# The first modulation of a two-block transformer found by four column tiles on TensorE, and GpSimd left out of the first four column blocks

## The chip, the cores and the metric

The kernel runs on one core of a Trainium2 chip. The metric is device time in microseconds of one execution. The profile is one execution, taken by the hardware profiler; its times count from the first instruction.

## The reference

Two transformer blocks work on x, [256 tokens, 1024 features], in float32. What matters here is the start of the first layer:

```python
mod = jax.nn.silu(c) @ ada_w + ada_b                 # [6144], from c [1024]
sh_m, sc_m, gt_m, sh_f, sc_f, gt_f = split(mod, 6)   # 1024 each
h = rms_norm(x, norm_mix) * (1 + sc_m) + sh_m        # rms_norm: x / sqrt(mean(x*x) + eps) * gain
proj = h @ w_in                                      # then attention, a gated delta net, ...
```

So before the first product `h @ w_in` can be finished, 2048 of the 6144 columns of `silu(c) @ ada_w` are needed (shift `sh_m`, scale `sc_m`): 8 MB of weights for one token's vector.

## The kernel before

x lies on chip by features: eight tiles X[k] of [128 features, 256 tokens]. Each float32 product is made of three float32r passes: a weight `w` is split into `wh` (rounded, by ScalarE, L193) and `wl` (the remainder, L194, by VectorE or GpSimd), and h likewise into `hh` and `hl`; L209, L210 and L211 are the three matmuls `wh hh`, `wh hl`, `wl hh`.

`begin0` starts the first layer. `Turn` squares X[k] on ScalarE (L65), adds the squares up on GpSimd (L67), and sums them over the features on TensorE (L81, tile `nps`); `rstd` (L290, L293) and `spread` (L271, L272) make 1 / rms, which ScalarE copies to `rb` (L465). Then four rounds j = 0..3 follow. Each round loads two units of ada_w (`mod_unit`, 1 MB each): VectorE multiplies [128 columns, 1024] by silu(c), which was spread over all partitions (`sc`, L458 and L459), and adds along the row (L346), twice a unit; L349 adds the bias, L352 makes the gain. The round also loads a weight block (0.5 MB) and cuts it, for j < 3 with the remainder on GpSimd; `norm` makes two blocks of h: the product with `rb` on GpSimd (L303), gain and shift on ScalarE (L305), `hh` on ScalarE (L308), `hl` on GpSimd (L309). Then TensorE multiplies what is there: in round j, weight blocks 0..j-1 with the two new blocks of h, and weight block j with all blocks of h so far.

Behind the four rounds `mixer1` goes on with token-major products (`pm`, L234 to L236), more column blocks (`pf`), convolutions (`gdn_conv`) and the gates' columns (`gps`, L658). A framework places the tiles and orders each engine's instructions ahead of time; on the chip each engine runs its own list strictly in that order, and waits where an operand isn't there. SyncE (SP) issues the loads in order too; a load waits until its buffer is free (five buffers for units of ada_w, three for weight blocks).

Of the kernel before, what the change touches and what calls it, by code (L numbers as in the profile page):

```python
# [17 lines left out]
P = 128          # partitions  # L18
S = 256          # tokens
SE = S + 2       # tokens and, beside them, columns for the shift  # L20
KT = 8           # feature blocks of the model width
NF = 22          # feature blocks of a feed-forward width
# [3 lines left out]
SENT = -3.4e38   # marks the scores that the top-64 search has taken  # L26

# columns of the packed constants
# [13 lines left out]
# columns of the packed norm gains: eight per norm  # L42
# [3 lines left out]
class Turn:  # L46
    """From one phase to the next.  step(k) follows the last update of x's feature block k and adds its squares;
    then(ms) follows the last of them, with the sums of each token, [128 tokens, 2]."""
# [48 lines left out]
class Start(Turn):  # L97
    """The next phase's h is x * gain, without the 1 / rms that all of x decides: that factor (net.rb along the free
    axis, net.rcol per partition) comes on the products, the first two of which run while it is found.  A shift rides
    along as columns beside the tokens: W' shift stands beside each product."""  # L100
# [42 lines left out]
class Net:  # L143
    """x lives on chip as eight [128 features, 256 tokens] tiles.  A float32 product is done as three
    float32r passes: both operands are split exactly into a rounded part and its remainder."""
# [29 lines left out]
    def parts(self, pool, name, n):  # L175
        """Two lists of a tile per feature block: the rounded parts and the remainders."""
        return [[pool.tile([P, n], F32R, name=f"{name}{i}{k}") for k in range(KT)] for i in "hl"]

# [18 lines left out]
    def split(self, src, hi, lo, scale=None):  # L197
        """hi + lo = src (times a column), both float32r."""
# [14 lines left out]
    def proj_fm(self, w, pool=None, tag="pj", n=S, between=None, h=None, bufs=2):  # L213
        """PSUM [128 columns, n] = W' h, for a [128, 8, 128] block of W."""
# [8 lines left out]
    def proj_tm(self, outs, src, n, pre=None):  # L223
        """outs[tb] [128 tokens, n] = h' W, for W as [2, 128, 4, n]."""
# [16 lines left out]
    def blocks(self, src, i0, n=2, pool=(), ws=None):  # L241
        """PSUM [128 columns, 256 tokens] of n blocks of columns."""
# [10 lines left out]
    def first(self, src, eng=None):  # L253
        """The first two blocks of a phase, loaded and split ahead."""
        ws = self.load(src, (P, 2, KT, P))
        return [self.cut(ws[:, j], eng=eng) for j in range(2)]

# [1 line left out]
    def warm(self, func, after):  # L259
        """Has the activation table of func loaded once the column `after` is there."""  # L260
# [3 lines left out]
    def spread(self, r, psum):  # L264
        """PSUM [128, 256]: r [128 tokens, 2] along the free axis, on every partition."""
# [9 lines left out]
    def rsqrt(self, y, x, t):  # L275
        """y = 1 / sqrt(x), by Newton's steps from the halved exponent, to float32's rounding."""
# [8 lines left out]
    def rstd(self, ms, eps=None, then=None):  # L285
        """1 / sqrt(ms / 1024 + eps); ms: [128 tokens, 2]."""
# [9 lines left out]
    def norm(self, ks, gain, shift, pool, act, rest):  # L296
        """h = x * rstd * gain + shift, split into hh + hl; gain and shift: [128, 8] columns.  The blocks whose product
        GpSimd does, whose gain and shift ScalarE, and whose remainder GpSimd: the others go to VectorE."""
# [12 lines left out]
    def final(self, ms, psum, gain, dst=None):  # L311
        """x = x * rstd * gain, kept or written out."""
# [13 lines left out]
    def two_norms(self):  # L326
        """The second block's first norm straight from the first block's x: with y = x g1 / sqrt(a + eps),
        a = mean(x^2), the norm of y is x g1 g2 / sqrt(mean(x^2 (g1^2 + eps)) + eps^2)."""
# [116 lines left out]
    def begin0(self, w_fm, pp):  # L445
        """The first layer's h by feature blocks, as their modulation comes in, and beside it four blocks of columns."""
        nc, tc, io = self.nc, self.tc, self.io
        with tc.tile_pool(name="st", bufs=1) as sp:
# [12 lines left out]
            for k in range(KT):  # L461
                t.step(k)
# [1071 lines left out]
```

## Time and profile before

| | |
|---|---|
| three timed runs | 1507.74, 1509.89, 1514.95 us |
| median | 1509.89 us |
| profiled execution, first to last instruction (its span) | 1508.1 us |
| TensorE matmuls busy in the span | 1429.1 us (95%) |
| VectorE, ScalarE, GpSimd busy | 1163.1, 841.9, 183.1 us |
| GpSimd busy from 18 to 46 us | 27.7 us of 28 |
| TensorE busy from 18 to 46 us | 9.7 us of 28 |

The profile gives the profiled execution no time of its own beside this span. Over the whole span TensorE is nearly always busy; the first 55 us are the exception, and the change lies there.

### The profile page before, as it was taken

How to read it: one execution, taken by the hardware profiler on the slowest of the kernel's cores; microseconds unless marked ns; L12 is line 12 of the kernel's file. 1: busy time of each engine (PE TensorE's matmuls, PEld its weight loads, DVE VectorE, ACT ScalarE, POOL GpSimd, SP SyncE). 2: the span in 40 equal slices, each digit the busy share in tenths (PEclk: the TensorE clock that was granted, in tenths of full speed). 3: DMA queues.
4: the chain of work that ended last, by engine and by line, in shares of the span. 5: the costliest groups of instructions: out<-in, count | busy, mean ns of one | idle time of the engine just before them, and what ended most of it. 6: DMA issues, size and time to landing. Idle time of an engine off the chain costs nothing.

```text
span 1508.1 us, 27966 instructions
## 1 busy us (share of the span) xinstructions
PE 1429.1 (95%) x11162; PEld 1350.4 (90%) x11162; DVE 1163.1 (77%) x2319; ACT 841.9 (56%) x1604; POOL 183.1 (12%) x164
## 2 busy tenths in 40 slices
PE   3888899999998899999999999999999999999998
PEld 2877789999997788999999988989999888899997
DVE  6879879999968565986567796698788665897875
ACT  3735775544465667654446555475555654765554
POOL 7434101000042410100001000110000100100000
PEclk9999999999999999999999999999999999999999
DMA  8567447898823522688844434179673332565520
GB/s 325 194 228 240 155 159 278 341 324 328 317 105 105 182 90 71 223 304 154 287 175 138 168 130 151 56 278 217 236 259 130 122 130 85 224 223 193 199 85 29
DMA packets 52500, 287.96 MB, mean 191 GB/s; under 512 B 6061, under 2 KB 11953, under 8 KB 24466
## 3 DMA queue, kind: packets, MB, share of 16 engines
q1 hardware_dynamic: 50962, 279.89, 50.8%
q0 software_dynamic: 1408, 6.29, 3.5%
q8 instruction: 87, 1.43, 0.4%
q14 instruction: 43, 0.35, 0.1%
HBM read 278.23 MB, written 7.34 MB: 189 GB/s over the span
## 4 chain that ended last, share of the span: by engine, by line
PE 76%; DVE 14%; POOL 4%; ACT 3%; issue 3%; DMA 1%; POOLq 0%; DVEq 0%; ACTq 0%
PE pf L209 14%; PE pf L210 14%; PE pf L211 14%; PE acc L209 5%; PE acc L211 5%; PE acc L210 5%; DVE wl L194 2%; DVE ws L346 2%; PE ot L415 2%; PE sc L377 2%; DVE hl L205 1%; POOL sq L67 1%; PE tp L408 1%; POOL h L303 1%; PE sc L376 1%
## 5 line engine op out<-in xcount | busy, mean ns | idle before, releaser
L210 PE MATMUL pf<-hl,wh 128*128 128x256 f32 (+1 forms) x2008 | 571.8, 285 | 12.3 <-DVE hl L205 7.3
L209 PE MATMUL pf<-hh,wh 128*128 128x256 f32 (+1 forms) x2008 | 576.8, 288 | 5.8 <-ACT hh L308 4.6
L211 PE MATMUL pf<-hh,wl 128*128 128x256 f32 (+1 forms) x2008 | 570.3, 285 | 10.9 <-POOL wl L194 9.2
L193 ACT CAST wh<-ws 128x1024 fp32r<-128x1024 f32 (+1 forms) x303 | 311.5, 1036 | 184.1 <-PE pf L210 133.8
L194 DVE TENSOR_TENSOR wl<-ws,wh 128x1024 fp32r<-128x1024 f32 (+1 forms) x290 | 356.1, 1231 | 70.5 <-ACT wh L193 69.2
L210 PEld LDWEIGHTS pf<-hl,wh 128*128 128x128 f32 x2008 | 382.9, 191 | 18.5 <-DVE hl L205 10.6
L211 PEld LDWEIGHTS pf<-hh,wl 128*128 128x128 f32 x2008 | 382.4, 191 | 12.4 <-POOL wl L194 9.8
L209 PEld LDWEIGHTS pf<-hh,wh 128*128 128x128 f32 x2008 | 382.4, 191 | 10.2 <-ACT hh L308 4.9
L211 PE MATMUL acc<-ah,dl 128*128 128x256 f32 x704 | 198.2, 282 | 0.0
L210 PE MATMUL acc<-al,dh 128*128 128x256 f32 x704 | 198.0, 282 | 0.0
L209 PE MATMUL acc<-ah,dh 128*128 128x256 f32 x704 | 197.7, 283 | 0.2
L67 POOL TENSOR_TENSOR sq<-sq 128x256 f32<-128x256 f32 x59 | 50.7, 859 | 786.4 <-ACT sq L65 780.3
L194 DVE TENSOR_TENSOR dl<-wd,dh 128x1024 fp32r<-128x1024 f32 x88 | 107.6, 1223 | 48.4 <-ACT dh L193 48.2
L193 ACT CAST dh<-wd 128x1024 fp32r<-128x1024 f32 x88 | 91.9, 1048 | 90.9 <-PE acc L210 87.5
L210 PEld LDWEIGHTS acc<-al,dh 128*128 128x128 f32 x704 | 133.7, 190 | 0.2
L211 PEld LDWEIGHTS acc<-ah,dl 128*128 128x128 f32 x704 | 133.6, 190 | 0.0
L209 PEld LDWEIGHTS acc<-ah,dh 128*128 128x128 f32 x704 | 132.9, 190 | 0.7 <-ACT ah L201 0.6
L346 DVE SCALAR_TENSOR_TENSOR ws<-ws,sc 128x1024 f32<-128x1024 f32 x96 | 121.4, 1278 | 4.7 <-DMA ws<-in_ada_w 4.7
L1069 DVE SCALAR_TENSOR_TENSOR fy<-fu,cw,fy 128x255 f32<-128x255 f32 (+1 forms) x176 | 84.1, 481 | 5.7 <-ACT fy L1067 3.0
L388 ACT ACTIVATE lg<-lg,st 128x128 f32<-128x128 f32 x112 | 49.8, 447 | 23.0 <-DVE st L383 15.4
L194 POOL TENSOR_TENSOR wl<-ws,wh 128x1024 fp32r<-128x1024 f32 x13 | 34.9, 2688 | 224.3 <-ACT wh L193 224.3
L1050 DVE TENSOR_TENSOR a<-pf,rb 128x258 f32<-128x258 f32 x88 | 37.1, 424 | 31.5 <-PE pf L211 29.3
(368 smaller groups left out, 2286.4 us busy)
## 6 DMA issues: line engine op xcount, KB each, us to landing
ws<-in_ada_w SPq DMA_DIRECT2D x48, 1024.0 KB, 6.4
ws<-in_w_gu SPq DMA_DIRECT2D x44, 1024.0 KB, 6.0
wd<-in_w_dn SPq DMA_DIRECT2D x44, 1024.0 KB, 6.7
ws<-in_w_up SPq DMA_DIRECT2D x44, 1024.0 KB, 4.8
ws<-in_w_fm SPq DMA_DIRECT2D x16, 1024.0 KB, 5.1
ws<-in_w_even SPq DMA_DIRECT2D x12, 1024.0 KB, 4.8
w<-in_cmp_w SPq DMA_DIRECT2D x8, 1024.0 KB, 4.8
ws<-in_w_out SPq DMA_DIRECT2D x8, 1024.0 KB, 4.8
```

The costliest lines, as they stand in the source:

```text
L67: (nc.vector if i else nc.gpsimd).tensor_tensor(sq, sq, last, op=ALU.add)
L193: nc.scalar.copy(wh, ws)
L194: (eng or nc.vector).tensor_tensor(wl, ws, wh.bitcast(F32), op=ALU.subtract)
L209: mm(out, lhsT=lh, rhs=rh, start=start, stop=False, **kw)
L210: mm(out, lhsT=lh, rhs=rl, start=False, stop=False, **kw)
L211: mm(out, lhsT=ll, rhs=rh, start=False, stop=stop, **kw)
L346: nc.vector.scalar_tensor_tensor(a, a, 1.0, self.sc, op0=ALU.mult, op1=ALU.mult, accum_out=acc)
L377: nc.tensor.matmul(sc[:, 128:384], lhsT=q[:, 128:256], rhs=kz, start=True, stop=True)
L388: nc.scalar.activation(lg[:, rng[i]], lg[:, rng[i]], AF.Exp, bias=nm[:, i:i + 1], scale=-1.0, accum_out=den[:, i:i + 1])
L415: mm(out, lhsT=v0, rhs=pt[:, 0:256], start=start, stop=False, skip_group_check=True)
L1050: nc.vector.tensor_tensor(t[j], ps[j], self.rb, op=ALU.mult)
L1069: nc.vector.scalar_tensor_tensor(y[:, d:S], u[:, 0:S - d], w[:, 2 - d:3 - d], y[:, d:S], op0=ALU.mult, op1=ALU.add)
```

## The change

Comments are left out. `io["ada_q"]` holds the first 2048 columns of ada_w of layer 0 again, in eight pieces of 1 MB with the 1024 inputs on partitions, so that they can be the moving operand of a matmul; a column of silu(c), padded to 32 columns with zeros (`cz`), is the stationary one. Each of the eight matmuls of a round takes one piece of 128 inputs and the same 512 columns (256 of the shift, 256 of the scale); the four of one load write to partitions 0, 32, 64 and 96 of one tile (`mrow`), the four of the second load add to them. A copy to SBUF and four matmuls with a column of ones (`mcol`) sum the four partial rows and turn them into columns.

```diff
+    def mod_rows(self, sp, pp, j, cz):
+        nc = self.nc
+        ps = pp.tile([P, 512], F32, tag="g", name="mrow", bufs=3)
+        for i in range(2):
+            aw = self.load(self.io["ada_q"][j, i], (P, 4, 512), sp, tag="aq", bufs=5)
+            for k in range(4):
+                q = slice(32 * k, 32 * k + 32)
+                nc.tensor.matmul(ps[q, :], lhsT=cz[:, 4 * i + k, :], rhs=aw[:, k, :], start=i == 0, stop=i == 1,
+                                 skip_group_check=True)
+        row = sp.tile([P, 512], F32, tag="mrow", name="mrow", bufs=2)
+        nc.scalar.copy(row, ps)
+        mp = pp.tile([P, 2, 2], F32, tag="s", name="mcol")
+        for i in range(4):
+            nc.tensor.matmul(mp[:, i // 2, i % 2:i % 2 + 1], lhsT=row[:, i * P:i * P + P], rhs=self.one, start=True,
+                             stop=True)
+        b = slice(2 * j, 2 * j + 2)
+        two = lambda t: t[:, 0, 0:16].rearrange("p (a b) -> p a b", a=2)[:, :, b]
+        nc.vector.tensor_tensor(two(self.mod), mp, two(self.adab), op=ALU.add)
+        nc.vector.scalar_tensor_tensor(self.gmod[:, 0, 0, b], self.mod[:, 0, 8 + 2 * j:10 + 2 * j], 1.0,
+                                       self.nrm[:, N_MIX + 2 * j:N_MIX + 2 * j + 2], op0=ALU.add, op1=ALU.mult)
...
     def begin0(self, w_fm, pp):
...
+            ct = sp.tile([P, KT], F32, name="ct")
+            nc.sync.dma_start(ct, io["c_cols"])
+            nc.sync.dma_start(self.x, io["x"])
             row = sp.tile([1, 1024], F32, name="row")
             nc.sync.dma_start(row, io["c"])
-            nc.sync.dma_start(self.x, io["x"])
             nc.sync.dma_start(self.adab, io["ada_b"])
             nc.sync.dma_start(self.nrm, io["norms"])
-            nc.sync.dma_start(self.cw, io["gdn_conv_w"])
-            for i in range(2):
-                t = slice(512 * i, 512 * i + 512)
-                ps = pp.tile([P, 512], F32, tag="g", name="cb", bufs=3)
-                nc.tensor.matmul(ps, lhsT=self.ones[0:1, :], rhs=row[:, t], start=True, stop=True)
-                nc.scalar.activation(self.sc[:, t], ps, AF.Silu)
-            t = Turn(self, (pp, "s", 2))
+            cz = sp.tile([P, KT, 32], F32, name="cz")
+            nc.vector.memset(cz, 0.0)
+            nc.scalar.activation(cz[:, :, 0], ct, AF.Silu)
+            t = Turn(self, (pp, "s", 2), cuts=range(KT - 1))
...
+            xr = sp.tile([P, KT, S], F32, name="xr")
+            for k in range(KT):
+                nc.vector.tensor_tensor(xr[:, k, :], self.X[k], self.rb[:, 0:S], op=ALU.mult)
...
             for j in range(4):
-                for u in (4 + j, j):
-                    self.mod_unit(0, u, sp)
-                w.append(self.cut(self.load(w_fm[j], (P, KT, P)), eng=nc.gpsimd if j < 3 else None))
-                self.norm((2 * j, 2 * j + 1), self.gmod[:, 0, 0, :], self.mod[:, 0, 0:8], range(8), range(8), range(8))
+                self.mod_rows(sp, pp, j, cz)
+                w.append(self.cut(self.load(w_fm[j], (P, KT, P))))
+                for k in (2 * j, 2 * j + 1):
+                    gain, shift = self.gmod[:, 0, 0, k:k + 1], self.mod[:, 0, k:k + 1]
+                    hh, hl = self.hh[k][:, 0:S], self.hl[k][:, 0:S]
+                    h = self.np.tile([P, S], F32, tag="h", name="h", bufs=2)
+                    nc.scalar.activation(hh, xr[:, k, :], AF.Identity, scale=gain, bias=shift)
+                    nc.vector.tensor_scalar(h, xr[:, k, :], gain, shift, op0=ALU.mult, op1=ALU.add)
+                    nc.vector.tensor_tensor(hl, h, hh.bitcast(F32), op=ALU.subtract)
...
+            nc.sync.dma_start(self.cw, io["gdn_conv_w"])
+            for i in range(2):
+                t = slice(512 * i, 512 * i + 512)
+                ps = pp.tile([P, 512], F32, tag="g", name="cb", bufs=3)
+                nc.tensor.matmul(ps, lhsT=self.ones[0:1, :], rhs=row[:, t], start=True, stop=True)
+                nc.scalar.activation(self.sc[:, t], ps, AF.Silu)
```

With `cuts=range(KT - 1)` each square goes to TensorE by itself: sixteen matmuls `nps` in place of two, and no adds on GpSimd. `sc`, which later units of the modulation still need, is made behind the four rounds.

The first place is TensorE's list in rounds 0 and 1. Before, from the sums of the squares (`nps`) through `rb` to the matmuls of round 0 and the start of round 1:

```order
L81 MATMUL nps<-one,sq 128x1 x2
L272 MATMUL rb<-d,ones 128x128 x2
L209 MATMUL pf<-hh_70,wh 128x256
L210 MATMUL pf<-hl_78,wh 128x256
L211 MATMUL pf<-hh_70,wl 128x256
L209 MATMUL pf<-hh_71,wh 128x256
L210 MATMUL pf<-hl_79,wh 128x256
L211 MATMUL pf<-hh_71,wl 128x256
```

And now at the same place (hh_70, hh_71 are blocks 0 and 1 of h, hl_78 and hl_79 their remainders):

```order
L81 MATMUL nps<-one,sq 128x1 x16
L272 MATMUL rb<-d,ones 128x128 x2
L454 MATMUL mrow<-aq,cz 32x512 x8
L460 MATMUL mcol<-one,mrow 128x1 x4
L209 MATMUL pf<-hh_70,wh 128x256
L210 MATMUL pf<-hl_78,wh 128x256
L211 MATMUL pf<-hh_70,wl 128x256
L209 MATMUL pf<-hh_71,wh 128x256
L210 MATMUL pf<-hl_79,wh 128x256
L211 MATMUL pf<-hh_71,wl 128x256
L454 MATMUL mrow<-aq,cz 32x512 x8
L460 MATMUL mcol<-one,mrow 128x1 x4
```

The twelve matmuls of the next round's modulation now stand in TensorE's list behind the last matmul of the round before, which needs that round's `hl`.

The second place is round 0 on the engine that makes the remainders. Before, GpSimd's list (h is x times `rb`):

```order
L303 TENSOR_TENSOR h<-x,rb 128x256 x2
L194 TENSOR_TENSOR wl<-ws,wh 128x1024
L309 TENSOR_TENSOR hl_78<-h,hh_70 128x256
L309 TENSOR_TENSOR hl_79<-h,hh_71 128x256
L303 TENSOR_TENSOR h<-x,rb 128x256 x2
```

Now VectorE's list, behind `rb`:

```order
L490 TENSOR_TENSOR xr<-x,rb 128x256 x8
L464 TENSOR_TENSOR mod<-mcol,adab 128x2x2
L465 SCALAR_TENSOR_TENSOR gmod<-mod,nrm 128x2
L502 TENSOR_SCALAR h<-xr,gmod,mod 128x256 x2
L194 TENSOR_TENSOR wl<-ws,wh 128x1024
L503 TENSOR_TENSOR hl_78<-h,hh_70 128x256
L503 TENSOR_TENSOR hl_79<-h,hh_71 128x256
L464 TENSOR_TENSOR mod<-mcol,adab 128x2x2
```

The same subtraction of the weight block stands ahead of `hl` on either engine; on VectorE all of it waits for `mod`, and so for `mcol`. From about the 300th matmul on TensorE's list is the same in both kernels.

## Rows read from the trace of the kernel before

**Rows 1.** Busy time by engine (window, length, busy us (count), clock, DMA share, GB/s).
```profile
20.00:30.00 10.00, 2.81 (x8) 1.93 (x8) 9.90 (x14) 3.14 (x6) 10.00 (x6) 1.00 1.00 414
```

**Rows 2.** Chain that ended last, rounds 0 and 1 (start us, us, what).
```profile
18.31 3.11 POOL h L303 x2
21.42 3.29 POOL wl L194
24.70 2.42 POOL hl L309 x2
...
33.82 2.42 POOL hl L309 x2
```

**Rows 3.** Timeline of TensorE, first of the token-major products (start us, us).
```profile
55.28 0.29 PE L234 MATMUL pm<-wh,hh 128*128 128x276 f32 x1
```

**Rows 4.** TensorE's waits from 55 to 130 us (total, times, longest).
```profile
PE gps L658 <- DVE ghbrk L734: 0.3, 1, 0.3
```

**Rows 5.** Timeline of the norm ahead of round 0 (idle before in brackets).
```profile
6.54 1.32 ACT L65 ACTIVATE sq<-x 128x256 f32<-128x256 f32 x4
...
14.64 1.01 PE L81 MATMUL nps<-one,sq 128*128 128x1 f32 x4 [8.63 <-POOL sq L67]
15.69 0.26 ACT L290 ACTIVATE r<-nps,eps 128x2 f32<-128x2 f32 x1 [2.62 <-PE nps L81]
...
16.60 1.22 PE L272 MATMUL rb<-d,ones 128*128 128x128 f32 x4 [0.95 <-DVE d L271]
```

**Rows 6.** Timeline of TensorE in round 3, where its matmuls become shorter.
```profile
45.42 0.58 PE L210 MATMUL pf<-hl,wh 128*128 128x256 f32 x1 [0.73 <-POOL hl L309]
...
47.94 0.41 PE L210 MATMUL pf<-hl,wh 128*128 128x256 f32 x1
...
48.15 0.41 PE L211 MATMUL pf<-hh,wl 128*128 128x256 f32 x1
...
48.54 0.28 PE L210 MATMUL pf<-hl,wh 128*128 128x256 f32 x1
...
48.66 0.28 PE L211 MATMUL pf<-hh,wl 128*128 128x256 f32 x1
```

**Rows 7.** Timeline of TensorE's weight loads for `cb` (512 float32 columns a record).
```profile
3.25 0.33 PEld L458 LDWEIGHTS cb<-row,ones 1*128 1x128 f32 x1 [0.52 <-issue]
4.10 0.33 PEld L458 LDWEIGHTS cb<-row,ones 1*128 1x128 f32 x1 [0.52 <-issue]
```

**Rows 8.** Chain, plain float32 matmuls later on: records of 1 and of 512 columns.
```profile
61.52 1.23 PE ssp L714 x12
...
72.39 1.72 PE dp L670 x4
```

**Rows 9.** Timeline of TensorE, column tiles of the compressed branch: 8 matmuls, 16 records.
```profile
98.87 1.05 PE L929 MATMUL hp<-w,win 128*15 128x256 f32 x16
```

**Rows 10.** A line's instructions: copies of 512 columns from PSUM (ns min/median/max).
```profile
L802 ACT COPY y<-yp x20: 564/586/592, 97.1 to 543.2; 128x512 f32<-128x512 f32 x20
```

**Rows 11.** Timeline of VectorE: a small gain, a weight remainder, a norm's steps in layer 1.
```profile
16.66 0.15 DVE L352 SCALAR_TENSOR_TENSOR gmod<-mod,nrm 128x2 f32<-128x2 f32 x1
...
46.99 1.21 DVE L194 TENSOR_TENSOR wl<-ws,wh 128x1024 fp32r<-128x1024 f32 x1
...
443.24 0.73 DVE L307 TENSOR_SCALAR h<-h,gmod,mod 128x256 f32<-128x256 f32 x2 [0.63 <-POOL h L303]
...
444.54 0.75 DVE L309 TENSOR_TENSOR hl<-h,hh 128x256 fp32r<-128x256 f32 x2
```

**Rows 12.** Busy time by engine at two later places (columns as in rows 1).
```profile
242.90:246.00 3.10, 2.99 (x14) 2.99 (x15) 2.20 (x5) 1.28 (x2) 0.00 (x0) 0.52 0.32 48
...
485.30:488.70 3.40, 3.22 (x15) 3.23 (x16) 1.24 (x5) 0.59 (x1) 0.00 (x0) 0.51 0.01 2
```

**Rows 13.** Timeline of TensorE just ahead of these two places.
```profile
242.14 0.39 PE L210 MATMUL pf<-hl,wh 128*128 128x258 f32 x1 [1.29 <-DVE hl L205]
...
485.48 1.12 PE L765 MATMUL xp<-ident,xt 128*128 128x128 f32 x4 [2.43 <-DVE xt L762]
```

More of the change, by code (lines that the diff above doesn't have):

```diff
@@ L448, in begin0 @@
         with tc.tile_pool(name="st", bufs=1) as sp:
+            ct = sp.tile([P, KT], F32, name="ct")
+            nc.sync.dma_start(ct, io["c_cols"])
+            nc.sync.dma_start(self.x, io["x"])
             row = sp.tile([1, 1024], F32, name="row")
             nc.sync.dma_start(row, io["c"])
-            nc.sync.dma_start(self.x, io["x"])
             nc.sync.dma_start(self.adab, io["ada_b"])
             nc.sync.dma_start(self.nrm, io["norms"])
+            cz = sp.tile([P, KT, 32], F32, name="cz")
[3 more added lines that the diff above has]
+            for k in range(KT):
+                t.step(k)
+            t.finish()
+            self.rcol = self.rstd(t.ms)
+            nc.scalar.copy(self.rb[:, 0:S], self.spread(self.rcol, (pp, "s", 2)))
+            xr = sp.tile([P, KT, S], F32, name="xr")
+            for k in range(KT):
+                nc.vector.tensor_tensor(xr[:, k, :], self.X[k], self.rb[:, 0:S], op=ALU.mult)
+            out = [self.pj.tile([P, S], F32, tag="pj", name="pf") for _ in range(2)]
+            out += [pp.tile([P, S], F32, tag="g", name="pf", bufs=3) for _ in range(2)]
+            w = []
+            for j in range(4):
+                self.mod_rows(sp, pp, j, cz)
[7 more added lines that the diff above has]
+                    nc.vector.tensor_tensor(hl, h, hh.bitcast(F32), op=ALU.subtract)
+                for b, (wh, wl) in enumerate(w):
+                    for k in range(2 * j if b < j else 0, 2 * j + 2):
+                        self.mm3(out[b], wh[:, k, :], wl[:, k, :], self.hh[k][:, 0:S], self.hl[k][:, 0:S],
+                                 k == 0, k == KT - 1)
             nc.sync.dma_start(self.cw, io["gdn_conv_w"])
@@ L459, in begin0 @@
                 nc.scalar.activation(self.sc[:, t], ps, AF.Silu)
-            t = Turn(self, (pp, "s", 2))
-            for k in range(KT):
-                t.step(k)
-            t.finish()
-            self.rcol = self.rstd(t.ms)
-            nc.scalar.copy(self.rb[:, 0:S], self.spread(self.rcol, (pp, "s", 2)))
-            out = [self.pj.tile([P, S], F32, tag="pj", name="pf") for _ in range(2)]
-            out += [pp.tile([P, S], F32, tag="g", name="pf", bufs=3) for _ in range(2)]
-            w = []
-            for j in range(4):
-                for u in (4 + j, j):
-                    self.mod_unit(0, u, sp)
-                w.append(self.cut(self.load(w_fm[j], (P, KT, P)), eng=nc.gpsimd if j < 3 else None))
-                self.norm((2 * j, 2 * j + 1), self.gmod[:, 0, 0, :], self.mod[:, 0, 0:8], range(8), range(8), range(8))
-                for b, (wh, wl) in enumerate(w):
-                    for k in range(2 * j if b < j else 0, 2 * j + 2):
-                        self.mm3(out[b], wh[:, k, :], wl[:, k, :], self.hh[k][:, 0:S], self.hl[k][:, 0:S],
-                                 k == 0, k == KT - 1)
         return out
@@ L1409, in _layout @@
     io["ada_w"] = a["ada_w"].transpose(0, 2, 1).reshape(2, 24, 2, P, 1024).transpose(0, 1, 3, 2, 4)
+    q = a["ada_w"][0, :, 0:2048].reshape(2, 4, P, 2, 4, 256)
+    io["ada_q"] = q.transpose(4, 0, 2, 1, 3, 5).reshape(4, 2, P, 4, 512)
+    io["c_cols"] = cols(a["c"][0])
     io["ada_b"] = cols(a["ada_b"])
```

## The prediction

> **What bounds the kernel now.** I read the busy times by engine first. In a stretch of the first rounds [rows 1] GpSimd is busy all 10.00 us and TensorE 2.81, while the DMA engines move 414 GB/s: either GpSimd or the loads could be the bound. The chain that ended last decides it: it runs through GpSimd's product, weight remainder and `hl`, 3.11 + 3.29 + 2.42 us and then the next product [rows 2]. From one `hl` pair to the next it is 33.82 - 24.70 = 9.12 us, and four such rounds bring TensorE to its first `pm` at 55.28 us [rows 3]. From there TensorE hardly waits: the wait for `gps` of 0.3 us [rows 4] is one of few before 90 us, and from about the 300th matmul on both kernels have the same list. So what the change is worth is how far that 55.28 moves, plus what is late behind it.
>
> **The norm.** Removed: the adds on GpSimd that hold TensorE until 14.64 us [rows 5]. Added: fourteen more `nps` matmuls, 28 records more. Four records take 1.01 us [rows 5], of which the last is some 0.37 long, so they start 0.21 us apart; eight squares of four records are 8 x 0.85 = 6.8 us. The squares begin at 6.54 [rows 5], now without the two `sc` activations ahead of them, so say 6.1 with the first done at 6.5: TensorE ends at 6.5 + 6.8 + 0.2 = 13.5. Before, the matmuls of `rb` ended at 16.60 + 1.22 = 17.82, 2.17 us behind the end of `nps` at 15.65 [rows 5]; that part is kept. Round 0 can begin on TensorE at 15.7. x is asked for second, as before: the small load of c in columns takes the place of the one in a row.
>
> **A round.** What it removes is GpSimd's 9.12 us. What takes its place is a serial chain, since `mrow` of a round stands on TensorE's list behind the last product of the round before, which needs that round's `hl`. I price it at both levels of TensorE's clock. In round 3 the fp32r matmuls start 0.21 us apart (47.94, 48.15), which is the 1.2 GHz level, and then 0.12 (48.54, 48.66), the 2.4 GHz level [rows 6]; the granted clock reads 1.00 in both, so I go by the spacing.
>
> - `mrow`: 8 matmuls are 16 records of 512 columns. One alone takes 0.85 us at 1.2 GHz [rows 7] and 1.72 / 4 = 0.43 at 2.4 [rows 8]. The trace has column tiles of the same build: 16 records of 256 columns in 1.05 us [rows 9], where one after the other would need 16 x 0.215 = 3.4; less 0.17 us of pipeline at the end that is 3.9 at a time. So `mrow` takes 16 x 0.85 / 3.9 + 0.2 = 3.7 us, or 1.9 at 2.4 GHz.
> - the copy on ScalarE 0.59 [rows 10], with a handover of 0.05 on each side 0.7.
> - `mcol`: 8 records, 8 x 0.21 + 0.15 = 1.85; at 2.4 GHz, where twelve take 1.23 [rows 8], 1.0.
> - VectorE: `mod` and `gmod` 0.15 each [rows 11], with handovers 0.4; two h 0.73, the weight remainder 1.21 and two `hl` 0.75 [rows 11]: 3.1 us until TensorE can use the last `hl`.
>
> Together 9.35 us at 1.2 GHz and 6.7 at 2.4. The steps of lines 464, 502 and 503 are not in the trace of before; the rows are those of the same forms on the same engine, and I see no reason for more than 0.5 us a round in either direction.
>
> Behind the last `hl` of a round TensorE still has 2, 9, 20 and 30 products to do before the next round's `mrow` (counted on its list): 61 at 0.215 or 0.12 us, 13.1 or 7.3. Then one `cb` matmul of two records, 1.7 or 0.9 (the other one fits into a wait).
>
> **The sum.** Everything from `mrow` of round 0 on at 1.2 GHz: 15.7 + 4 x 9.35 + 13.1 + 1.7 = 67.9 us. All at 2.4 GHz: 15.7 + 26.8 + 7.3 + 0.9 = 50.7. Before: 55.28. So the clock decides the sign.
>
> What did it do before? It rose at about 48.4 us, when TensorE had worked without a pause since 45.42 [rows 6]. It then held until two places where TensorE had paused for 1.29 and for 2.43 us [rows 13]; behind each the granted clock is 0.5, the lower level, for some microseconds of dense work [rows 12]. A round of the changed kernel is a dense stretch (products, then `mrow`), and then 4.5 us with little in them: the copy, `mcol` of one column each, and VectorE's 3.1 us. So I expect the clock to fall in each of these, and to rise again only near the end of a dense stretch. Rounds 0 and 1, with 3.7 and 4.1 us of dense work, at 1.2 GHz: 15.7 + 9.35 + 0.4 + 9.35 + 1.9 = 36.7. Round 2: the nine products and `mrow` are 5.6 us without a pause, the clock rises in them and saves about 0.9 of `mrow` and 0.85 of `mcol`: 7.6; its 20 products start low again, 4.3: 48.6. Round 3 saves all of `mrow` and `mcol`, 6.7, and of the 30 products half run low: 15 x 0.215 + 15 x 0.12 = 5.0, `cb` 0.9: 61.2. If one of the short stretches of round 0 or 1 already lifts the clock, it is up to 3 us less. I take 60.5, 5.2 us later than 55.28.
>
> Hidden: the loads. Eight units and two weight blocks more would keep the DMA engines busy to about 30 us as before; the sixth unit now waits until TensorE has read the first (about 17.6 us) and the last pair is asked for at about 28, needed at 48. Without that cover a unit of 1 MB costs 1.05 MB / 414 GB/s = 2.5 us. VectorE's eight products `xr` (8 x 0.375 = 3 us by the `hl` rows) lie beside `mrow` of round 0. A second table load for Silu on ScalarE lies beside the 30 products. Behind `pm`, VectorE begins the convolutions about 3 us later than before relative to `pm`, since it now cuts five weight pieces first; the wait for `gps` [rows 4] may grow from 0.3 us to 2: I take 0.3 more.
>
> The forecast is 5.5 us longer: the profiled span of 1508.1 becomes 1513.6. The median of the runs lies 1.8 us above that span, so 1515 us.
>
> **A rule against the row.** By [rows 9] four column tiles give 3.9 at a time. The Trainium skill (page "TensorE: Matmul & The Clock Gate", section "Measured speedup vs the span model") has 2.38 times for three column tiles of 512 columns; four at that rate would be 3.2 times, an estimate from the page, `mrow` then 4.5 us at 1.2 GHz, and the total by the page some 3 us more, 1518 us. I go by the row, which is this kernel's own pattern.
>
> **Rivals.**
> 1. *The clock stays up from the first `mrow` on.* For it: TensorE is busier in these rounds than before, and it held 2.4 GHz from 48.4 us on for almost 200 us. Against: the falls behind pauses no longer than those here [rows 13]. It gives 50.7 us, 4.6 less than before, 1505.5 us; if the squares run at 2.4 GHz too, 3.4 less still, 1502. This is the case on the other side: all of the work after 15.7 us at 1.2 GHz costs 17.2 us more than at 2.4, so it decides once two thirds of that work run at 2.4 GHz. The same page's section "Why this matters for your kernels" says that only longer pauses between bursts drop the clock; by that rule this rival is the result. The row of 1.29 us does not bear it out. Chance 0.17.
> 2. *The clock never rises before round 3's products.* Then 67.9 less about 2 us at the end, 66: 10.5 us more than before, 1521. For it: in rounds 0 to 2 of the kernel before it never rose. Against: waits for GpSimd broke up TensorE's work there, and here nine and then twenty products run into `mrow` without one. Chance 0.13.
> 3. *The column tiles run one after the other* (a new accumulation in each, 512 columns). `mrow` is then 13.6 us at 1.2 GHz, 6.9 at 2.4; so long a stretch lifts the clock, some 9 us, 5.5 more in each round: 1537. Against it stand [rows 9]. Chance 0.04.
>
> **How the numbers follow.** The forecast has 0.66; its own range is 2 to 9 us longer, 1512 to 1519 (bounds: 57.5 to 62.5 us at `pm`, 0 to 2 behind it). To leave out no more than two in ten, the range reaches down to the first rival, 1504, and up to the second, 1522. Half a per cent, 7.5 us, is about what a measurement can tell from no change. Faster by more needs nearly all of rival 1 with the squares: 0.09. Slower by more: the upper part of the forecast, 0.15, and rivals 2 and 3: 0.32. Within: 0.59.
>
> **What would show it.** In the changed profile the first `pm` should start near 60 us; `mrow` of round 0 near 15.7; sixteen `mrow` records in 3.7 us in rounds 0 and 1; 3.1 us from `mcol`'s end to the last `hl`'s use; no wait of TensorE for loads after round 0; GpSimd idle from 3 us to the rotary products. I am wrong if `mrow` takes 1.9 us in every round, if the serial chain is broken (`mrow` of a round overlapping VectorE's work of the round before), or if `pm` moves and the time does not, which would mean a later wait has absorbed it.

## The result and the profile after

Four runs of the changed kernel took 1515.47 to 1519.5 us, median 1517.82; four of the kernel before beside them 1506.41 to 1514.95, median 1508.82. The ratio is 1.0055 with a 95% interval of 0.0035 to 0.0074 above one: slower by about half a per cent. The forecast was 1515. The profiled execution took 1516.56 us with a span of 1514.8, 6.7 more than the span of before.

Where the time went is read from the first start of a few tiles on TensorE, in the order of the program: `pm`, the decays `dp`, the compressed branch `hp`, the attention output `ot`, the first and the last accumulation `acc` of the feed-forward parts.

| first start, us | pm | dp | hp | ot | acc | last acc | span |
|---|---|---|---|---|---|---|---|
| before | 55.28 | 72.23 | 91.64 | 121.15 | 255.93 | 1497.95 | 1508.1 |
| after | 59.88 | 77.52 | 98.31 | 127.99 | 260.50 | 1504.08 | 1514.8 |
| difference | 4.60 | 5.29 | 6.67 | 6.84 | 4.57 | 6.13 | 6.7 |

So 4.6 us are lost ahead of `pm` and 2.1 between `pm` and `hp`. Behind `hp` the difference does not simply stay: for the same matmul it goes down from 6.9 to 3.0 us, mostly where TensorE's clock falls in the kernel before (243 and 485 us, [rows 12]), and up to 6.1 where it falls in the changed one (636 us). That the spans end 6.7 us apart, as `hp` does, is in part luck.

The chain of waits after, from round 0 to round 2 (start us, us, what):

```profile
22.96 0.44 DVE hl L503
...
24.87 3.62 PE mrow L454 x16
...
28.51 0.59 ACT mrow L457
...
29.15 1.07 PE mcol L460 x8
...
30.63 0.61 ACT hh L501
...
31.28 1.23 DVE wl L194
...
32.55 0.58 PE pf L211
...
35.93 1.90 PE mrow L454 x16
```

Where GpSimd stood in every line before [rows 2], the work now goes round in a circle: TensorE's `mrow`, ScalarE's copy, TensorE's `mcol`, VectorE, then TensorE's products, and only then the next `mrow`. For the most part one engine works while the others wait. The weight remainder `wl`, which needs nothing of the round, stands in the middle of the circle. VectorE's timeline has the idle time in brackets, 6.52 us ahead of round 1's `mod`:

```profile
30.24 0.16 DVE L464 TENSOR_TENSOR mod<-mcol,adab 128x4 f32<-128x4 f32 x1 [6.52 <-PE mcol L460]
```

The four `mrow`, the wait for `wl` in round 1 and the first `pm` on TensorE's timeline (start us, us):

```profile
15.70 3.28 PE L454 MATMUL mrow<-aq,cz 128*32 128x512 f32 x16
...
24.80 3.64 PE L454 MATMUL mrow<-aq,cz 128*32 128x512 f32 x16
...
32.55 0.58 PE L211 MATMUL pf<-hh,wl 128*128 128x256 f32 x1 [0.89 <-DVE wl L194]
...
35.86 1.92 PE L454 MATMUL mrow<-aq,cz 128*32 128x512 f32 x16
...
46.74 1.93 PE L454 MATMUL mrow<-aq,cz 128*32 128x512 f32 x16
...
59.88 0.39 PE L234 MATMUL pm<-wh,hh 128*128 128x276 f32 x1
```

And the granted clock over the rounds (columns as in rows 1; the number behind the bracket of POOL is the clock, 0.50 is 1.2 GHz):

```profile
21.90:28.70 6.80, 5.48 (x22) 1.91 (x22) 1.82 (x4) 0.56 (x2) 0.00 (x0) 0.50 0.93 342
28.70:32.10 3.40, 1.83 (x11) 1.43 (x11) 1.79 (x5) 2.43 (x4) 0.00 (x0) 1.00 0.97 404
32.10:35.50 3.40, 2.95 (x14) 2.95 (x15) 1.07 (x3) 0.00 (x0) 0.00 (x0) 0.51 0.66 196
35.50:42.30 6.80, 4.58 (x34) 2.53 (x34) 2.60 (x7) 2.62 (x4) 0.00 (x0) 1.00 0.01 5
42.40:45.70 3.30, 3.30 (x18) 3.30 (x17) 0.17 (x1) 0.00 (x0) 0.00 (x0) 0.50 0.73 230
45.80:52.60 6.80, 5.92 (x40) 3.18 (x38) 2.01 (x5) 3.20 (x6) 0.00 (x0) 1.00 0.00 0
```

The clock rises once in each round, towards the end of the dense stretch of products and `mrow`, and is down again when VectorE's part of the round is over. So `mcol` finds it up and most of the products find it down. The loads were no limit: no wait of TensorE from 15 to 60 us ends with one, and from 35.5 to 42.3 us next to nothing was moved (last column).

### The profile page after: what moved, and what is told of

It reads as the page before. It is cut to its first block, busy times and chain, and to the rows that moved or that the text cites. A ratio compares the mean times of both kernels' runs of the same rounds, so it can differ in the third digit from the quotient of the medians.

```text
span 1514.8 us, 28187 instructions
## 1 busy us (share of the span) xinstructions
PE 1450.3 (96%) x11286; PEld 1363.4 (90%) x11286; DVE 1144.8 (76%) x2311; ACT 842.7 (56%) x1602; POOL 145.6 (10%) x138
## 4 chain that ended last, share of the span: by engine, by line
PE 76%; DVE 15%; ACT 3%; issue 2%; POOL 1%; DMA 1%; POOLq 0%; SPq 0%; DVEq 0%; ACTq 0%
PE pf L211 14%; PE pf L209 14%; PE pf L210 14%; PE acc L209 5%; PE acc L211 5%; PE acc L210 5%; DVE wl L194 3%; DVE ws L346 2%; PE ot L415 2%; PE sc L377 1%; DVE hl L205 1%; PE tp L408 1%; POOL sq L67 1%; PE sc L376 1%; PE nps L81 1%
## 5 line engine op out<-in xcount | busy, mean ns | idle before, releaser
L67 POOL TENSOR_TENSOR sq<-sq 128x256 f32<-128x256 f32 x52 | 44.2, 851 | 779.2 <-ACT sq L65 773.6
L346 DVE SCALAR_TENSOR_TENSOR ws<-ws,sc 128x1024 f32<-128x1024 f32 x80 | 101.9, 1283 | 1.4 <-DMA ws<-in_ada_w 1.2
L1104 ACT ACTIVATE fy<-fu,cw 128x256 f32<-128x256 f32 x88 | 52.6, 599 | 12.1 <-DVE fu L1103 11.9
```

The lines of the kernel that those rows point to most:

```text
L67: (nc.vector if i else nc.gpsimd).tensor_tensor(sq, sq, last, op=ALU.add)
L346: nc.vector.scalar_tensor_tensor(a, a, 1.0, self.sc, op0=ALU.mult, op1=ALU.mult, accum_out=acc)
L1104: nc.scalar.activation(y, u, AF.Identity, scale=w[:, 2:3], bias=w[:, 3:4])
```

## The experiments

From the place that the changed kernel reaches at about 80 us on, TensorE's list is the same in all kernels, tile by tile. The table gives what was measured; each run is told below. Ratios are to the kernel before, run beside it.

| run | first pm | first hp | span | median of runs | ratio, 95% interval |
|---|---|---|---|---|---|
| changed kernel | 59.88 | 98.31 | 1514.8 | 1517.82 | 1.0055 (1.0035 to 1.0074) |
| a_wl_first | 53.53 | 91.70 | 1506.1 | 1509.42 | 1.0000 (0.9982 to 1.0018) |
| b_pipe | 45.77 | 87.20 | 1505.4 | 1504.41 | 0.9976 (0.9960 to 0.9992) |
| c_warm | 54.60 | 92.92 | 1512.8 | 1511.63 | 1.0020 (1.0005 to 1.0036) |
| d_unit_dve | 49.87 | 86.28 | 1503.3 | 1505.36 | 0.9973 (0.9959 to 0.9988) |
| e_rows_pool | 64.85 | 103.12 | 1520.1 | 1522.16 | 1.0081 (1.0063 to 1.0098) |
| f_sums_pool | 62.50 | 100.83 | 1521.4 | 1523.18 | one run |
| g_one_tile | 71.11 | 108.91 | 1521.7 | 1523.51 | one run |
| i_best | 42.86 | 85.04 | 1502.6 | 1504.38 | 0.9965 (0.9953 to 0.9978) |
| j_sc_first | 60.21 | 95.88 | 1509.6 | 1513.93 | 1.0026 (1.0011 to 1.0041) |
| k_best2 | 44.25 | 80.55 | 1498.3 | 1500.47 | 0.9929 (0.9908 to 0.9949) |

In b and g a few `pm` stand ahead of the last products on TensorE's list (39.30 and 66.80 us); the table has the first behind them.

The theory is a serial chain, with about half of TensorE's work in it at the lower clock. The rivals: it is the clock alone; it is the work that VectorE took over from GpSimd; it is the column tiles; it is something behind `pm`.

**a_wl_first: VectorE's part of the chain made shorter,** and the new weight block's products with the old blocks of h put beside it.

```diff
-                self.mod_rows(sp, pp, j, cz)
-                w.append(self.cut(self.load(w_fm[j], (P, KT, P))))
+                ps = self.mod_rows(sp, pp, j, cz, aws)
+                w.append(self.cut(ws))
+                self.mod_cols(sp, pp, j, ps)
...
+                    for k in range(2 * j):
+                        self.mm3(out[j], wh[:, k, :], wl[:, k, :], self.hh[k][:, 0:S], self.hl[k][:, 0:S], k == 0, False)
```

> The list order of VectorE, ScalarE and TensorE is written out by hand in the four rounds: each weight block is cut (wh, wl) before the round's mod, and TensorE does the new block's products with the old blocks of h while VectorE makes the new h. mrow of a round still stands behind the last product of the round before. Theory (a serial chain through VectorE, half of it at the lower clock): VectorE's share of a round falls from 3.1 to 1.9 us, 4.8 us over four rounds, and 17 or more products move out of the tail into VectorE's time, 2 to 3.6 us: the first pm starts at 52 us (50.5 to 54) instead of 59.88, and the time is 1510 us (1507 to 1513). Rival, the lower clock alone: pm 57 or later, since mrow of the first two rounds stays at 3.3 to 3.7 us. Rival, loads or GpSimd's absence: pm stays within 1.5 us of 59.9.

Measured: 53.53 us and 1509.42, as fast as the kernel before. VectorE's part is 1.94 us in round 0 (from 21.44 to 22.48 + 0.90) and as much in rounds 1 and 2. The clock still goes up and down: `mrow` takes 3.64, 3.13, 2.00 and 1.92 us. But it is down for less of the time, so the 6.35 us that come back at `pm` are not the chain's alone. Busy time by engine from 15.7 us to `pm` (columns as in rows 1), of the changed kernel and of a:

```profile
15.70:59.88 44.18, 35.70 (x198) 23.29 (x197) 17.90 (x41) 16.08 (x24) 0.00 (x0) 0.81 0.60 218
...
15.70:53.53 37.83, 33.44 (x199) 21.34 (x198) 18.25 (x41) 16.17 (x24) 0.00 (x0) 0.86 0.70 261
```

TensorE's idle time falls from 8.5 to 4.4 us: these 4.1 us are the chain's, shorter and with products in what was a wait. The other 2.3 us are busy time, for the same work at a higher mean clock. The rival of the clock alone, `pm` at 57 us or later, falls. The timeline of a, VectorE in round 0 and TensorE's first `pm`:

```profile
21.44 0.16 DVE L469 TENSOR_TENSOR mod<-mcol,adab 128x4 f32<-128x4 f32 x1 [1.02 <-PE mcol L465]
...
22.48 0.90 DVE L512 TENSOR_TENSOR hl<-h,hh 128x256 fp32r<-128x256 f32 x2
...
53.53 0.40 PE L234 MATMUL pm<-wh,hh 128*128 128x276 f32 x1
```

**b_pipe: the chain broken.**

```diff
+            rows[0] = self.mod_rows(sp, pp, 0, cz, aws)
             for j in range(4):
+                if j < 3:
+                    rows[j + 1] = self.mod_rows(sp, pp, j + 1, cz, aws)
...
+                if j < 3:
+                    self.mod_cols(sp, pp, j + 1, rows[j + 1])
```

> As the run with wl first, and mrow of round j+1 stands on TensorE's list ahead of round j's products, and mcol of round j+1 inside them, so that VectorE's work of one round lies beside TensorE's of the next. Theory (serial chain): TensorE hardly pauses from 16 us on, the clock rises once before 25 us and stays; the work left is 20 us at 2.4 GHz and some 3 us more for the part at 1.2; the last unit of ada_q has landed by about 32 us: first pm at 40 us (38 to 43), time 1499 us (1495 to 1503), about 10 us less than before. Rival, the clock alone: pm near 54. Rival, what comes behind pm (convolutions, gate columns, loads of w_misc and of the next blocks) takes the gain back: pm near 40 but the first hp less than 8 us earlier than the 98.3 us it has in the changed kernel, and the time within 4 us of 1517.8.

Measured: 45.77 us and 1504.41; too optimistic by 6 us at `pm` and by 5 in time. TensorE does work nearly all of 15 to 45 us, 28.15 of 30 us where the changed kernel has 22.64 (busy time by engine, columns as in rows 1):

```profile
15.00:45.00 30.00, 28.15 (x201) 18.72 (x202) 18.73 (x41) 14.53 (x23) 0.00 (x0) 0.94 0.87 338
```

so the chain was what kept it idle. Two things were missed in what was expected. The clock fell once more in round 2, and `mrow` took 3.56 us there. And 14.1 us at `pm` became 11.1 at `hp`: TensorE waits 1.24 us for the gates' columns, and behind that wait the decays run at the lower clock, 3.40 us against 1.88 in the changed kernel. TensorE's timeline there:

```profile
62.67 0.36 PE L714 MATMUL gps<-gg,cs 128*128 128x8 f32 x2 [1.24 <-DVE gcols L781]
...
63.80 3.40 PE L726 MATMUL dp<-ug,cs 128*128 128x512 f32 x4
```

**c_warm: the clock alone.** The added matmuls change nothing that is read.

```diff
+            def fill(n):
+                for _ in range(n):
+                    tc.keep_in_program_order(nc.tensor.matmul(dp, lhsT=dr[:, 0:P], rhs=dr, start=True, stop=True))
...
+                fill(4)
...
+                fill(8)
```

> The changed kernel with 12 more float32r matmuls of 256 columns on ones in each round, four behind mrow and eight behind mcol, where TensorE waits; they write to a tile that nobody reads. The chain is untouched, only the clock may change. Theory: rounds 0 and 1 lose 1.4 and 1.7 us of mrow to the lower clock, and some 45 of the 61 trailing products lose 0.095 each, 4.3 us: with the clock up throughout the first pm starts near 53.5 us (52 to 56), time 1512 us. Rival, the clock does not set it: pm stays at 59 to 62 us. Rival, the clock is all of it: pm at 50.7 us or less.

Measured: 54.60 us and 1511.63, with everything 0.66 us later from the start (`mrow` of round 0 at 16.36). The granted clock reads 1.00 in the whole stretch (busy time by engine, columns as in rows 1):

```profile
16.00:54.60 38.60, 35.47 (x248) 24.28 (x246) 16.90 (x40) 15.79 (x24) 0.00 (x0) 1.00 0.64 240
```

but at its beginning that can't be taken at its word, as in [rows 6]: `mrow` of round 0 took 3.64 us, the lower level. From round 0's `mcol` on (1.05 us) the lengths are those of the upper level, and `mrow` of rounds 1 to 3 takes 1.92 us, as here in round 1 on TensorE's timeline:

```profile
25.24 1.92 PE L454 MATMUL mrow<-aq,cz 128*32 128x512 f32 x16
```

So the lower clock behind round 0's `mrow` is worth 59.88 - 54.60 + 0.66 = 5.9 us, and without it the changed kernel would have had its `pm` at 53.9 us, 1.3 earlier than before instead of 4.6 later. In time that would not have been a gain: c is still 0.2% slower than the kernel before, with its later start and the loss behind `pm`, which the clock leaves as it was (38.3 us to `hp`). Its rounds 1 to 3 last 8.0, 9.4 and 12.0 us from `mrow` to `mrow` or `pm`; the prediction's terms at 2.4 GHz give 6.7 + 1.1 = 7.8, 6.7 + 2.4 = 9.1 and 6.7 + 3.6 + 0.9 = 11.2.

**d_unit_dve and e_rows_pool: the two parts of the change one at a time.** d keeps the modulation on VectorE and takes GpSimd out; e puts the modulation on TensorE and leaves GpSimd its work. d makes `sc` at the start, as before; e makes it behind the rounds, as the changed kernel does.

```diff
d:
-                self.mod_rows(sp, pp, j, cz)
+                for u in (4 + j, j):
+                    self.mod_unit(0, u, sp)
e:
-                w.append(self.cut(self.load(w_fm[j], (P, KT, P))))
+                w.append(self.cut(self.load(w_fm[j], (P, KT, P)), eng=nc.gpsimd if j < 3 else None))
...
+                self.norm((2 * j, 2 * j + 1), self.gmod[:, 0, 0, :], self.mod[:, 0, 0:8], range(8), range(8), range(8))
```

> Only the part of the change that takes GpSimd out: the modulation by VectorE (two units a round, sc at the start) as before, but x / rms formed once on VectorE, h, hl and wl on VectorE, sixteen nps matmuls. VectorE then has some 8.2 us a round (four products with sc at 1.15, wl 1.15, xr, h and hl 0.7 each pair, small ones 0.4), but three of the eight units are done before rb is there; from 17.5 us on 26 us of VectorE's work and the products of round 3, 5 us: first pm near 49 us (47 to 53), 6 us less than before, time 1503 us. Theory: the loss comes from the modulation on TensorE. Rival, the loss comes from giving GpSimd's work to VectorE: pm at 58 us or later, time 1513 us or more.

> Only the part of the change that moves the modulation to TensorE: mrow and mcol as in the changed kernel, but GpSimd adds the squares, forms h times rb, wl of rounds 0 to 2 and hl as before. Theory (serial chain): a round is mrow 1.9 to 3.7, copy 0.7, mcol 1.05, mod and gmod 0.4, gain, shift and hh on ScalarE some 1.5, hl on GpSimd 2.4, then the products; GpSimd's own 8.8 us a round bound it from below: first pm at 61 us (58 to 65), time 1519 us (1515 to 1523), that is no better than the whole change. Rival, GpSimd's absence is what costs: pm 57 us or less.

Measured: d 49.87 us and 1505.36, faster than before by 0.27%; e 64.85 us and 1522.16, slower by 0.81%. So GpSimd's absence is a gain, though VectorE is then busy 26.76 of 27 us, and the modulation on TensorE, laid out as it is here, is the loss, with what the late `sc` costs in it: the rival that blames VectorE's new work falls. Busy time by engine in d (columns as in rows 1), the one before the clock being GpSimd's:

```profile
18.00:45.00 27.00, 12.29 (x57) 10.92 (x57) 26.76 (x60) 7.27 (x11) 0.00 (x0) 1.00 0.65 253
```

In e one reason given was wrong: GpSimd did not bind from below. With VectorE nearly idle its `wl` takes 2.34 us (3.29 in [rows 2]) and a pair of `hl` 1.42 (2.42 there). A round is 11.6 us long (`mrow` starts at 25.79 and 37.40 us) because the circle now has GpSimd's `wl` in it, behind which even the `gmod` of two columns on VectorE is held until `wl` ends. The timeline of GpSimd and VectorE in round 1 of e:

```profile
30.18 2.34 POOL L194 TENSOR_TENSOR wl<-ws,wh 128x1024 fp32r<-128x1024 f32 x1 [3.80 <-ACT wh L193]
...
30.50 2.04 DVE L465 SCALAR_TENSOR_TENSOR gmod<-mod,nrm 128x2 f32<-128x2 f32 x1
```

**f_sums_pool: the squares added on GpSimd again** (the argument `cuts` left out).

> The changed kernel with the squares added on GpSimd again (two nps matmuls). Theory: the norm ends 1.6 us later (before: 17.82, less 0.4 for the two activations that are no longer ahead of the squares, against 15.77), and all behind it moves along: mrow of round 0 starts at 17.3 us, first pm at 61.5 us (60 to 63, the clock adds up to 1 us either way). Rival, loads set the start of round 0 or of later rounds: pm unchanged at 59.9.

Measured: 62.50 us, in the expected range, but not by the expected path. The adds took 5.52 us where the kernel before took 7.25, `rb` ended 0.96 us later than in the changed kernel, not 1.6, and the framework put half of `mrow` ahead of `rb`, so `mcol` of round 0 was 0.54 us earlier. The other 3 us at `pm` go with the clock: from 15.7 us to `pm` its mean is 0.74 here and 0.81 in the changed kernel, and `mrow` of round 2 took 2.85 us in place of 1.92. The run prices the norm's part at 1 us or less; it doesn't settle more. GpSimd's timeline:

```profile
7.13 5.52 POOL L67 TENSOR_TENSOR sq<-sq 128x256 f32<-128x256 f32 x7 [4.46 <-ACT sq L65]
```

**g_one_tile: no column tiles.**

```diff
-                q = slice(32 * k, 32 * k + 32)
-                nc.tensor.matmul(ps[q, :], lhsT=cz[:, 4 * i + k, :], rhs=aw[:, k, :], start=i == 0, stop=i == 1,
+                self.tc.keep_in_program_order(nc.tensor.matmul(ps[0:32, :], lhsT=cz[:, 4 * i + k, :], rhs=aw[:, k, :],
+                                                               start=i + k == 0, stop=i + k == 4))
```

> The changed kernel without column tiles: the eight matmuls of a round's mrow all accumulate on partitions 0 to 31 of one tile, and the copy and mcol read 32 partitions. Theory (column tiles run four at a time): mrow takes 16 records of 0.43 us, 6.9 us, where the clock is up and 13.6 where it is low; so long a dense stretch lifts the clock in its course, so 8 to 11 us in round 0 and 7 to 9 later, 5 to 6 us a round more than now: first pm near 82 us (77 to 90). If four column tiles gave only three at a time, one tile would still give these lengths and mrow in the changed kernel would have been 2.3 us where it was 1.90. Rival, records of column tiles follow each other anyway: mrow unchanged at 1.9 to 3.6 us, pm near 60 us.

Measured: `mrow` 8.03, 8.74, 7.05 and 7.05 us, as expected; at the upper level 7.05 against 1.92 is 3.7 times for four column tiles, ends included. The forecast of `pm`, 82 us, missed by 11. Two things go with that: the framework put `wl` ahead of `mod` on VectorE's list here, as in a_wl_first, and the granted clock stayed at 1.00 from 31.8 us on, so that the products ran at the upper level. How the 11 us divide between them was not tested. TensorE's timeline in round 2:

```profile
41.94 7.05 PE L453 MATMUL mrow<-aq,cz 128*32 128x512 f32 x16
```

**i_best: the start moved earlier too.** b_pipe, with the squares added on VectorE (four `nps` records) and `mrow` of round 0 in halves around `rb`.

```diff
-            t = Turn(self, (pp, "s", 2), cuts=range(KT - 1))
+                t = Turn(self, (pp, "s", 2))
+                t.vec = True
...
+                ps = self.mod_rows(sp, pp, 0, cz, aws, part=(0,))
+                nc.scalar.copy(self.rb[:, 0:S], self.spread(self.rcol, (pp, "s", 2)))
+                self.mod_rows(sp, pp, 0, cz, aws, ps, (1,))
```

> The pipelined rounds, and the squares added up on VectorE (four nps records in place of 32), the first half of mrow of round 0 put between nps and rb, wh and wl of a weight block behind the round's hh and hl. Theory: in the pipelined run TensorE is the bound from 15.9 us on, so what starts earlier ends earlier, until the loads bound it: rb ends near 13.4 us instead of 16.0, mrow of round 0 near 15.3 instead of 19.4, the last unit of ada_q lands near 29 us, mrow of round 3 ends near 31.5 instead of 34.7, dp 3 us earlier than the 63.8 us of the pipelined run, time 3 us below its 1504.4: 1501.5 us (1499 to 1504). Rival, loads bound the pipelined run already: dp within 1 us of 63.8, time unchanged.

Measured: the start moved by less than expected (`rb` ends at 14.76, not 13.4; `mrow` of round 0 at 16.43, not 15.3, 2.9 us earlier than in b_pipe), `pm` came 2.9 us earlier, `dp` 0.5, and 1504.38 us is nothing gained in time. That is the sign the rival named, but the loads are only a part of it: they now end two waits in rounds 2 and 3, 1.38 and 0.85 us, and behind `pm` the gates' columns make TensorE wait 1.16 us and the decays then run at the lower clock again. TensorE's timeline at these places:

```profile
25.00 1.07 PE L457 MATMUL mrow<-aq,cz 128*32 128x512 f32 x8 [1.38 <-DMA aq<-in_ada_q]
...
31.24 1.06 PE L457 MATMUL mrow<-aq,cz 128*32 128x512 f32 x8 [0.85 <-DMA aq<-in_ada_q]
...
60.62 0.57 PE L733 MATMUL gps<-gg,cs 128*128 128x8 f32 x2 [1.16 <-DVE gg L722]
...
63.31 3.62 PE L745 MATMUL dp<-ug,cs 128*128 128x512 f32 x4
```

**j_sc_first and k_best2: what is late behind `pm`.** In the changed kernel, a, c, e and f, which make `sc` behind the rounds, `hp` starts 38.2 to 38.4 us behind `pm` (37.8 in g); in the kernel before and in d, which make it first, 36.4. In the changed kernel ScalarE's list shows why: `sc` waits for `cb`, which stands behind the products of round 3 on TensorE, and the convolutions' copy `cu` stands behind `sc`. Its timeline, and VectorE's:

```profile
59.98 0.60 ACT L514 ACTIVATE sc<-cb 128x512 f32<-128x512 f32 x1 [1.05 <-PE cb L513]
60.48 0.64 ACT L719 COPY cu<-pf 128x256 f32<-128x256 f32 x2
...
61.56 1.67 DVE L730 SCALAR_TENSOR_TENSOR kT<-cu,cw,kT 128x255 f32<-128x255 f32 x4 [1.37 <-ACT kT L728]
```

j is the changed kernel and k is i_best, each with `sc` back at the start:

```diff
             nc.sync.dma_start(ct, io["c_cols"])
-            nc.sync.dma_start(self.x, io["x"])
             row = sp.tile([1, 1024], F32, name="row")
             nc.sync.dma_start(row, io["c"])
+            nc.sync.dma_start(self.x, io["x"])
...
             nc.scalar.activation(cz[:, :, 0], ct, AF.Silu)
+            for i in range(2):
+                t = slice(512 * i, 512 * i + 512)
+                ps = pp.tile([P, 512], F32, tag="g", name="cb", bufs=3)
+                nc.tensor.matmul(ps, lhsT=self.ones[0:1, :], rhs=row[:, t], start=True, stop=True)
+                nc.scalar.activation(self.sc[:, t], ps, AF.Silu)
```

> The changed kernel with sc (two cb matmuls and two Silu activations) made at the start again, ahead of the squares, as before; the small load of c in a row goes ahead of x's. In the traces so far the first hp comes 36.4 us behind the first pm where sc is made at the start (before, and the run with the modulation on VectorE) and 38.2 to 38.4 where it is made behind the rounds. Theory of the late part: ScalarE's list has sc ahead of the convolutions' copies cu, and sc waits for cb, which TensorE reaches behind the 30 products of round 3, so the convolutions begin 3.5 us later against pm. With sc first: the squares 0.5 us later, two cb of 1.05 us out of the tail: first pm at 58.6 us (57.5 to 60), first convolution about 2 us ahead of pm instead of 1.7 behind it, first hp 36.4 us behind pm, 95 us, 3.3 less than in the changed kernel; time 3 us less, 1515 us (1512 to 1517). Rival, the remainders wl on VectorE's list (the prediction's reason): hp stays 38.3 us behind pm, 97 us.

> The pipelined rounds with the squares added on VectorE, and sc at the start. Theory (in the run before, what pm gained was lost behind it, where ScalarE's list holds sc and table loads ahead of the convolutions' and gates' steps): the squares 0.5 us later but the loads bound rounds 2 and 3, so the last products stay where they were; pm 1 us earlier than 42.86, the convolutions 2 to 3 us earlier, dp near 60.5 us instead of 63.3, hp near 82.5 instead of 85.0; time 1501.5 us (1499 to 1504) instead of 1504.4. Rival, VectorE or the loads of the later blocks bound the stretch from pm to hp: hp within 1 us of 85, time unchanged at 1504.

Measured: j has `pm` at 60.21 us, no earlier although the two `cb` left the tail; the mean clock from 15.7 us to `pm` is 0.77 here against 0.81, which can have hidden their gain. But `hp` comes 35.7 us behind `pm`, at 95.88, 2.8 us sooner than in the changed kernel. The time, 1513.93 us, moved the same way, though the intervals of the two ratios overlap. TensorE's waits from `pm` to `hp` (total, times, longest) show where this lies, first in the kernel before, then in the changed one:

```profile
PE xp L765 <- DVE xt L762: 0.8, 1, 0.8
PE gps L658 <- DVE ghbrk L734: 0.3, 1, 0.3
...
PE xp L802 <- DVE xt L799: 1.6, 1, 1.6
PE gps L695 <- DVE gcols L283: 0.8, 1, 0.8
PE pf L209 <- DVE ctv L944: 0.5, 1, 0.5
```

VectorE is late there, by 1.7 us more than before; in j the only wait left is 0.5 us, for `xt`. The convolutions start 2.4 us ahead of `pm`, by the timeline of ScalarE and VectorE in j:

```profile
56.22 0.37 ACT L719 COPY cu<-pf 128x256 f32<-128x256 f32 x1 [1.73 <-issue]
...
57.83 0.99 DVE L730 SCALAR_TENSOR_TENSOR kT<-cu,cw,kT 128x255 f32<-128x255 f32 x2
```

k gains where i didn't: TensorE no longer waits for the gates' columns, `dp` runs at the upper clock (1.88 us), `hp` starts at 80.55 us, and 1500.47 us is 0.7% below the kernel before: the fastest of all. Its `pm` is later than in i (44.25 against 42.86) although `cb` left the tail: the clock stayed low until round 2. TensorE's timeline in k:

```profile
17.59 1.87 PE L467 MATMUL mcol<-one,mrow 128*128 128x1 f32 x8 [0.70 <-ACT mrow L464]
19.38 3.64 PE L457 MATMUL mrow<-aq,cz 128*32 128x512 f32 x16
...
59.59 1.88 PE L745 MATMUL dp<-ug,cs 128*128 128x512 f32 x4
```

## Why the prediction was right, point by point

- **What bounds the kernel.** Right: what follows the fourth round moved with it, though the equal difference of 6.7 us at `hp` and in the spans is in part luck (see above).
- **The norm.** Right: `nps` 7.0 us from 6.61 (6.8 from 6.5), round 0's `mrow` at 15.70 (15.7).
- **`mrow`.** Right: 3.64 us in round 1 and 1.92 in rounds 2 and 3 (3.7 and 1.9); round 0's took 3.28, as the clock rose in it. g shows the column tiles to be worth 3.7 times. The Trainium skill, page "TensorE: Matmul & The Clock Gate", section "Measured speedup vs the span model", would have led to 7.05 / 3.2 = 2.2 us here, by the estimate of 3.2 times that the prediction made from its figure for three; the row of this kernel's own pattern was the better guide.
- **`mcol`.** Mis-sized in rounds 0 and 1: 1.05 us, not 1.85, because the clock was already up when it came. The low price itself was right: 1.87 in k, where the clock was down.
- **VectorE's part.** Right in length: 2.97 us from the end of `mcol` to the end of the last `hl` in round 1 (3.1). But in rounds 1 to 3 the last `hl` was not what TensorE waited for: its last wait was for `wl` (0.89, 0.77 and 0.36 us), and the products queued behind that. From the end of `mcol` to the next `mrow` round 1 took 5.66 us, where the prediction's terms give 3.1 + 1.9 = 5.0.
- **The clock.** Right in kind: it fell in each round's pause and rose in each dense stretch, and products ran at 0.21 us apart until 35.5, 45.6 and 56.0 us. It rose in rounds 0 and 1 already, which the forecast had at the lower level throughout. The ends of the rounds, 35.86, 46.74 and 59.88 us, stand against 36.7, 48.6 and 61.2, of which the prediction took 60.5. That is closer than the single terms came, which is luck in part: up to the end of `mcol` the four rounds took 2.7 us less than its terms, and from there to the next `mrow` or `pm` 1.4 us more. Rival 1 was wrong on the point named against it: in the rounds no pause of TensorE ahead of a fall was longer than 1.08 us, shorter than those of [rows 13], and c, which fills some of these pauses, shows what staying up would have given. The balance point named with it is off: (67.9 - 55.28) / 17.2 is nearer three quarters of the work than two thirds.
- **Loads hidden.** Right; they come to the surface only in i, where TensorE runs 3 us ahead of them.
- **Behind `pm`.** The step that failed. The prediction had VectorE late "since it now cuts five weight pieces first" and took 0.3 us for the wait for `gps`. That wait grew by about as much, from 0.3 to 0.75 us, but TensorE then waited for VectorE at two later places as well, and the whole was 2.1 us. The cause was another, too: not VectorE's list, where the first convolution step waited 1.37 us for ScalarE, but ScalarE's, where `sc` stood ahead of `cu`. The prediction priced `cb` on TensorE (0.9 us) and the second table load as hidden, and did not ask who stands behind `sc` on its own engine. j, which moves `sc` (with c's small load) and leaves the five pieces where they are, brings back 2.8 of `hp`'s 38.4 us behind `pm`.
- **The sum.** 4.6 us at `pm` (forecast 5.2) and 2.1 behind it (0.3): 6.7 us in the span, against 5.5. A term too long and one too short helped each other. The medians are 9.0 us apart; the 2.3 us beyond the profiles were not tied to a place. The two executions have TensorE's clock down at different later places ([rows 12] in the one, about 155 and 640 us in the other), and single runs of the kernel before spread over 8 us.

Not settled: how the 6.7 us divide. a, c and j give back 6.35 us at `pm`, 5.9 at `pm` and 2.8 behind it, each alone. The three overlap: of a's 6.35 us, 2.3 are TensorE's work at a higher mean clock.

## What to carry to other kernels

A stage that hops from engine to engine must be laid out so that the next round's first hop stands ahead of this round's last on its engine's list; taking the busiest engine out of such a stage does little when what replaces it is a circle. Price every moved step on each engine that it touches, and name who stands behind it there: here a small activation moved out of the way on TensorE held up the convolutions on ScalarE. And where TensorE works in bursts, work the sum out at both clock levels first, since the level can decide the sign, as it did here at `pm`.

## What the runs showed of the hardware

- Work without a pause did not always leave TensorE's clock up: the 32 `nps` records, of one column each, kept TensorE busy from 6.61 to 13.6 us, and `mrow`, from 15.7 us on, still began at the 1.2 GHz level (3.28 us in the changed kernel, 3.64 in c, which is later by 0.66).
- GpSimd and VectorE hold each other up far more than their busy times tell. VectorE's `gmod` of two columns took 2.04 us and ended with GpSimd's `wl` (e), and 0.16 alone; GpSimd's seven adds took 7.25 us beside VectorE's products with `sc` (before) and 5.52 without (f). The Trainium skill, page "SBUF — State Buffer", section "Summary: rules for kernel authors", says that where a VectorE instruction has two inputs in SBUF and GpSimd's reads SBUF, the second to issue is blocked until the first ends; the 2.04 us agree. It fits with taking GpSimd out (d) having paid although VectorE had more to do: VectorE's adds of the bias to two columns, from 15 to 46 us, took this in the kernel before and in d (ns min/median/max):

```profile
L349 DVE TENSOR_TENSOR mod<-mod,adab x7: 160/574/2184, 16.1 to 40.8; 128x2 f32<-128x2 f32 x7
...
L349 DVE TENSOR_TENSOR mod<-mod,adab x8: 151/154/158, 16.1 to 44.8; 128x2 f32<-128x2 f32 x8
```

- A wait of 1.2 us can be followed by a larger cost than its own: behind it, in b and i, the clock was down and the four decays `dp` took 3.40 and 3.62 us; in k, without the wait, 1.88. That the wait brought the clock down is argued from these three runs, not shown alone; behind 0.75 us, in the changed kernel, `dp` took 1.88.
